# A decode step for a prompt and a sample group: the sample group's HGRN step among the compressed branch's tiles, its state products in float32, and page-table loads issued later

## The chip, the core and the metric

One core of a Trainium2 chip runs the whole kernel. The metric is device time in microseconds (us) of one execution. The engines are TensorE (PE in the profile), VectorE (DVE), ScalarE (ACT), GpSimd (POOL) and SyncE (SP); SP, ACT and POOL each have a queue from which DMAs are issued.

## What is computed

One layer of a hybrid decoder: eight attention heads with three branches (compressed blocks, selected blocks, window) beside four HGRN heads with a state of 128 x 128 each. It runs for a prompt of 1024 tokens and for a sample group of 8 sequences with one new token each and 1024 earlier tokens in paged caches. The step that the change moves is the sample group's HGRN step, one chunk of length 1:

```
f = lb + (1 - lb) * sigmoid(f_b);  k = (1 - lb) * sigmoid(-f_b)
q = silu(q_b);  v = i_b
S_new = f[k] * S + k (x) v          # (8 sequences, 4 heads, 128, 128)
o = q @ S_new
y_b = rmsnorm(o) * norm_w * silu(z_b)
```

The compressed branch reads the raw K and V rows of each sequence through the page table (`cache_cmp_kv[page_table]`), forms overlapping blocks of 32 rows and sends each through a small two-layer network:

```
flat = (blocks + pe).reshape(B, nc, KVH, 32 * 64)
k_c, v_c = silu(flat @ w1 + b1) @ w2
```

## The kernel before

The program is one long stream of operations; a scheduler of the framework places them into one instruction order for each engine, from data dependences, the buffers of pools and the order in which the code emits them. Each engine runs its order strictly, so an instruction that waits holds back all behind it. `after(a, b)` (L44) adds an order between two instructions without a semaphore.

The stages are: loading and normalising x (`load_x`), the projections (`project`), the compressed branch, the maxima and the branches of the prompt's attention, the sample group's attention, and the finish. A projection multiplies x by a 128-row tile of weights in three F32R products (high by high, low by high, high by low), `feat` with 344 streamed columns; `load_w` (L224) loads a tile `w_raw` through SP, ACT makes `w_hi` (L238) and DVE `w_lo` (L239).

Into the projections are laid the prompt's four HGRN heads. `hgrn_a` builds the decay-weighted products of Q and K in PSUM and copies them through masks into the tile AT on DVE (L490, L513, L520, L540); `hgrn_b` multiplies AT by V, carries the state and normalises O (L608 on POOL), which PE then transposes (L612).

The sample group's step is the generator `hgrn_sample` (L422 to L467). `go` lets it run two heads between `hgrn_a` and `hgrn_b` of head 3 and one after it. For each head it loads the state S for eight sequences (128 partitions x 1024) and vb, the new v spread over 128 partitions from the DRAM tile v_d, both through SP (L437, L439). DVE forms vb*k (L441), POOL S*f (L442), DVE the sum (L443), and SP stores the new state (L444). ACT and DVE then split S into a high and a low F32R half (S0h, S0l), and eight pairs of matmuls against qp, a zero tile with q of one sequence in one column, add up o in PSUM. After the last head o is normalised and transposed (L464). All its tiles lie in the pool of the HGRN stage (hp), which is closed at `hctx.close()` before the compressed branch can use the memory.

`page_index` (L645) loads the page table in eight small DMAs (pt_raw, L651; 16 partitions x 8 elements of 4 bytes each) and makes the row index pidx on DVE (L658), which the gathers read.

The compressed branch (`compress_setup`, `compress`, L666 to L755) loads nine tiles of raw rows into `cg`, two buffers of 128 x 2048: eight by indirect DMA on POOL (`gather`, L660), tile 8 from the DRAM tile kv_d by SP (L706). DVE and ACT copy each out of its slot (cr, L710). It goes through three groups of three tiles, eight steps each; a step has a turn (six transposes on PE, L717, a high and a low half x on ACT and DVE) and a multiplication with w1 (12 matmuls), and each turn stands one step ahead of its multiplication. POOL subtracts the low halves w1l of the weights (L51). Projections (`feat` C_Q, C_ZA, C_ZB) fill PE in between.

Of the kernel before, what the change touches and what calls it, by code (L numbers as in the profile page):

```python
# [20 lines left out]
NB = 8  # L21
# [6 lines left out]
class Kernel:  # L28
# [44 lines left out]
    def rsqrt(self, pool, y, x):  # L73
# [3 lines left out]
        t = pool.tile([128, n], F32, name="rs_t")[:p]  # L77
        g = pool.tile([128, n], F32, name="rs_g")[:p]
# [19 lines left out]
    def consts(self):  # L98
# [23 lines left out]
        self.vcS = cp.tile([64, NB + 1, 128], F32, name="vcS")  # L122
# [101 lines left out]
    def load_w(self, src, *parts):  # L224
# [4 lines left out]
        for k in range(8):  # L229
            raw = self.wpool.tile([128, 512], F32, name="w_raw", bufs=3)[:, :width]  # L230
            o = 0
            for c0, n in parts:
                dma = nc.sync.dma_start(raw[:, o:o + n], src[k * 128:(k + 1) * 128, c0:c0 + n])
                o += n
# [45 lines left out]
    def project(self, ctx):  # L280
# [24 lines left out]
        def ev_f(h0):  # L305
            def ev(f, ts, p):
# [8 lines left out]
                nc.vector.tensor_scalar(K[h][:, ts], K[h][:, ts], self.oml[:, h:h + 1], None, op0=OP.mult)  # L315
# [74 lines left out]
        for _ in smp:  # L390
            pass
# [30 lines left out]
    def hgrn_sample(self):  # L422

        nc, hp, a = self.nc, self.hp, self.a
# [3 lines left out]
        o = hp.tile([32, 128], F32, name="so", bufs=1)  # L428
        for h in range(4):
            yield  # L430
            po = self.ps_t.tile([128, 512], F32, name="pt")[:64, :128]
            qp = hp.tile([128, NB, 64], F32R, name="qp", bufs=1)
            nc.vector.tensor_scalar(qp.rearrange("p (a c) d -> p a (c d)", c=2), self.ones[:, None, :].to_broadcast([128, 4, 128]), 0.0, None, op0=OP.mult)
            qv = qp.rearrange("p b c -> p (b c)")
            self.split(qv[:, h * NB:h * NB + 456:65], qv[:, 32 + h * NB:32 + h * NB + 456:65], q[:, h], nc.vector, nc.vector)
            S = hp.tile([128, NB, 128], F32, name="S0", tag="S")
            nc.sync.dma_start(S, a["state_hgrn"][0, :, h].rearrange("b k v -> k b v"))  # L437
            vb = hp.tile([128, NB, 128], F32, name="vb", tag="O")
            nc.sync.dma_start(vb, bass.AP(tensor=v_d.tensor, offset=v_d.offset + h * 128, ap=[[0, 128], [512, NB], [1, 128]]))  # L439
# [5 lines left out]
            hi = hp.tile([128, NB, 128], F32R, name="S0h", tag="F")  # L445
            lo = hp.tile([128, NB, 128], F32R, name="S0l", tag="F")
            self.split(hi, lo, S, nc.scalar, nc.vector)
            for b in range(NB):
                self.mm(po, qp[:, b], hi[:, b], b == 0, False)
                self.mm(po[:32], qp[:, b, :32], lo[:, b], False, b == NB - 1)  # L450
            if h:
                nc.vector.tensor_tensor(o, o, po[:32], op=OP.add)
            else:
                nc.vector.tensor_copy(o, po[:32])
            nc.vector.tensor_tensor(o, o, po[32:], op=OP.add)
        sq = hp.tile([32, 128], F32, name="ssq", bufs=1)
# [188 lines left out]
    def page_index(self, pool):  # L645
# [749 lines left out]
```

## Time and profile before

| | us |
|---|---|
| three runs | 1084.05, 1085.75, 1096.07 |
| median | 1085.75 |
| the profiled execution | 1086.7 |
| its span | 1085.0 |
| PE busy in the span | 1047.7 |

The span is that from the first to the last instruction of the trace; 1.7 us of the profiled execution lie around it. Busy time of PE counts matmuls whose ends are modelled. "Granted clock" is the mean share of full speed that TensorE was given in a stretch. In the rows, `out<-in` names tiles, `xN` counts instructions, and an arrow in brackets names what ended the idle time before an instruction.

### The profile page before, as it was taken

The numbers are of one execution on the slowest core, as the hardware profiler recorded it, in microseconds if no ns is written. First come the engines' busy times: TensorE is split into PE (matmuls) and PEld (weight loads), VectorE is DVE, ScalarE is ACT, GpSimd is POOL, SyncE is SP. The second block draws the span as 40 slices with busy tenths as digits, with TensorE's granted clock in tenths as the row PEclk, the third lists the DMA queues.
The fourth block names the chain that finished last, engine by engine and source line by source line (L and its number), as shares of the span: only waits on it lengthen the run. The fifth ranks groups of instructions, "written<-read, shape, count | busy, mean of one in ns | idle before, by whom it ended". The sixth has DMA issues, their size and how long they took to land.

```text
span 1085.0 us, 18918 instructions
## 1 busy us (share of the span) xinstructions
PE 1047.7 (97%) x7021; PEld 933.6 (86%) x7021; DVE 617.8 (57%) x1822; ACT 388.4 (36%) x786; POOL 243.9 (22%) x276
## 2 busy tenths in 40 slices
PE   4999999999899999999989999999999999999998
PEld 3898799999889899999968888888788888778876
DVE  6847565665494634543665656766665686471223
ACT  4622234313132335432234544553554232241112
POOL 0014232331041133002032211121323133131111
PEclk9999999999989999999989999999999999999999
DMA  6212023323464766403568611001831573121110
GB/s 195 79 29 69 11 72 100 117 89 119 131 176 142 214 210 211 148 1 107 129 215 266 154 29 51 20 21 53 227 106 40 161 209 90 41 97 49 49 35 30
DMA packets 118815, 116.44 MB, mean 107 GB/s; under 512 B 18710, under 2 KB 100974, under 8 KB 116420
## 3 DMA queue, kind: packets, MB, share of 16 engines
q1 hardware_dynamic: 97220, 79.46, 25.7%
q10 hardware_dynamic: 19200, 19.01, 5.1%
q0 software_dynamic: 2304, 16.78, 4.5%
q8 instruction: 55, 0.90, 0.4%
q14 instruction: 36, 0.29, 0.1%
HBM read 84.84 MB, written 29.31 MB: 105 GB/s over the span
## 4 chain that ended last, share of the span: by engine, by line
PE 82%; DMA 9%; DVE 4%; issue 2%; ACT 2%; POOL 1%; SPq 0%; ACTq 0%; DVEq 0%; POOLq 0%
PE pa L42 39%; PE pb L42 26%; PE ph L42 9%; PE pt L42 4%; DMA vb<-v_d 2%; DMA w_raw<-w_in 2%; PE ph L717 1%; PE pa L1125 1%; DMA fw_raw<-w_out 1%; DMA fw_raw<-ple_gate 1%; DMA x_in<-x_prompt 1%; DVE fw_lo L51 1%; PE ph L1319 1%; DMA gpre<-g_pre 0%; DMA f_oa<-oa_d 0%
## 5 line engine op out<-in xcount | busy, mean ns | idle before, releaser
L42 PEld LDWEIGHTS pb<-V,P 128*128 128x128 f32 x1056 | 141.8, 191 | 12.1 <-POOL P L960 1.2
L42 PE MATMUL pb<-V,P 128*128 128x128 f32 x1056 | 148.1, 276 | 0.4 <-DVE mx L909 0.4
L42 PE MATMUL pa<-xhi,w_hi 128*128 128x344 f32 x384 | 126.0, 330 | 2.6 <-ACT w_hi L238 1.1
L42 PE MATMUL pa<-xlo,w_hi 128*128 128x344 f32 x384 | 124.5, 326 | 0.0
L42 PE MATMUL pa<-xhi,w_lo 128*128 128x344 f32 x384 | 123.5, 327 | 0.0
L955 ACT ACTIVATE P<-ph 128x512 f32<-128x512 f32 (+4 forms) x148 | 85.6, 595 | 98.6 <-PE ph L42 69.3
L916 DVE CUSTOM_DVE_ANT_0 junk<-pa,mask 128x320 bf16<-128x320 f32 (+5 forms) x150 | 72.9, 497 | 27.8 <-PE pa L42 26.6
L42 PE MATMUL pa<-w_lo,xhi 128*128 128x256 f32 (+2 forms) x256 | 79.5, 314 | 0.0
L42 PE MATMUL pa<-w_hi,xlo 128*128 128x256 f32 (+2 forms) x256 | 79.2, 314 | 0.0
L42 PE MATMUL pa<-w_hi,xhi 128*128 128x256 f32 (+2 forms) x256 | 78.6, 316 | 0.0
L42 PEld LDWEIGHTS pa<-xhi,w_hi 128*128 128x128 f32 x384 | 73.5, 192 | 4.2 <-ACT w_hi L238 1.7
L238 ACT ACTIVATE w_hi<-w_raw,gpre 128x512 fp32r<-128x512 f32 (+2 forms) x80 | 47.5, 616 | 78.2 <-DMA w_raw<-w_in 43.0
L42 PEld LDWEIGHTS pa<-xlo,w_hi 128*128 128x128 f32 x384 | 73.5, 192 | 0.1
L42 PEld LDWEIGHTS pa<-xhi,w_lo 128*128 128x128 f32 x384 | 73.0, 191 | 0.2
L42 PE MATMUL ph<-QA,KA 128*128 128x512 f32 (+4 forms) x148 | 66.7, 453 | 3.8 <-ACT P L955 2.9
L42 PE MATMUL pa<-KB,QB 65*128 65x320 f32 (+6 forms) x195 | 63.4, 363 | 0.1
L239 DVE SCALAR_TENSOR_TENSOR w_lo<-w_raw,gpre,w_hi 128x512 fp32r<-128x512 f32 (+2 forms) x80 | 50.6, 653 | 21.4 <-ACT w_hi L238 20.7
L42 PE MATMUL pa<-fw_hi,yh 128*128 128x512 f32 (+1 forms) x160 | 61.9, 387 | 0.2 <-ACT fw_hi L50 0.2
L42 PE MATMUL pa<-fw_lo,yh 128*128 128x512 f32 (+1 forms) x160 | 61.6, 385 | 0.0
L42 PE MATMUL pa<-fw_hi,yl 128*128 128x512 f32 (+1 forms) x160 | 61.6, 385 | 0.0
L42 PE MATMUL ph<-QB,KB 68*128 68x512 f32 (+4 forms) x148 | 58.5, 406 | 0.0
L559 POOL TENSOR_TENSOR K<-K,E 128x512 f32<-128x512 f32 x24 | 36.4, 1517 | 94.2 <-PE pb L42 57.2
(457 smaller groups left out, 2411.9 us busy)
## 6 DMA issues: line engine op xcount, KB each, us to landing
w_raw<-w_in SPq DMA_DIRECT2D x32, 256.0 KB
w_raw<-w_in SPq DMA_DIRECT2D x48, 128.0 KB
VS<-sg SPq DMA_DIRECT2D x8, 512.0 KB
sg<-cache_win_kv SPq DMA_DIRECT2D x16, 256.0 KB
fw_raw<-w_out SPq DMA_DIRECT2D x16, 256.0 KB
fw_raw<-ple_gate SPq DMA_DIRECT2D x16, 256.0 KB
f_x<-x_prompt SPq DMA_DIRECT2D x8, 512.0 KB
win_kv_sample<-cache_win_kv SPq DMA_DIRECT2D x8, 511.0 KB
```

The source lines that it names most:

```text
L42: return self.nc.tensor.matmul(out, lhsT, rhs, start=start, stop=stop, skip_group_check=True)
L51: lo_eng.tensor_tensor(lo, src, hi.bitcast(F32), op=OP.subtract)
L238: nc.scalar.activation(hi, raw, AF.Copy, scale=g)
L239: nc.vector.scalar_tensor_tensor(lo, raw, g, hi.bitcast(F32), op0=OP.mult, op1=OP.subtract)
L559: nc.gpsimd.tensor_tensor(Kv[:, :, 0], Kv[:, :, 0], Ev[:, :, 1:2].to_broadcast([128, nb, m]), op=OP.mult)
L717: nc.tensor.transpose(pt[:, i * 128:(i + 1) * 128], src[b0 + j // 2, kv][:, j % 2, 2 * jp:2 * jp + 2].rearrange("p j d -> p (j d)"), self. ...
L916: nc.vector.tensor_tensor_reduce(junk, pm, mk, 1.0, -1e30, op0=OP.add, op1=OP.max, accum_out=o)
L955: nc.scalar.activation(P, ps, AF.Exp, scale=0.125)
L1125: nc.tensor.transpose(pt[:, j * 128:(j + 1) * 128], rows(j), self.ident)
L1319: nc.tensor.transpose(pt[:, c], h[:, k * 128:(k + 1) * 128], self.ident[:n, :n])
```

## The change

Three things are done. First, the generator `hgrn_sample` is cut into `update` and `read` for a head, and these are called from the loop over the compressed branch's steps: update 0, update 1, read 0, read 1 at steps 1 to 4, and update 2, update 3, read 2, read 3 at steps 9, 10, 12 and 13; the normalisation follows after the last step. S and vb of a head lie together in one slot of `cg`, and both are loaded through POOL's queue (L440, L441). Second, S is no longer split: qp (32 columns, float32, in a slot of `w1r`) is multiplied with S itself, one float32 matmul for each of the eight sequences. Third, the eight page-table loads are ordered behind the last weight load of the i projection, and the making of pidx (now `page_rows`) behind the last K of the f projection (`lastf`).

```diff
@@ load_w
-                dma = nc.sync.dma_start(raw[:, o:o + n], src[k * 128:(k + 1) * 128, c0:c0 + n])
+                dma = self.lastw = nc.sync.dma_start(raw[:, o:o + n], src[k * 128:(k + 1) * 128, c0:c0 + n])
@@ project
         self.feat((C_FB + 256, 2, ev_f(2)))
+        self.page_rows()
         self.feat((C_QB + 256, 2, ev_q(2)))
-        go = lambda n: [next(smp, None) for _ in range(n)]
         for h in range(2, 4):
-            st = self.hgrn_a(h, Q[h], K[h], F[h])
-            go(2 if h == 3 else 0)
-            self.hgrn_b(h, *st)
-            go(1 if h == 3 else 0)
+            self.hgrn_b(h, *self.hgrn_a(h, Q[h], K[h], F[h]))
...
-        for _ in smp:
-            pass
...
             comp = self.compress()
-            for _ in range(5):
-                next(comp)
-            self.feat((C_Q, 4, ev_qa))
+
+            i = 0
             for _ in comp:
+                if i in (1, 2, 3, 4, 9, 10, 12, 13):
+                    next(smp, None)
+                if i == 4:
+                    self.feat((C_Q, 4, ev_qa))
+                i += 1
+            for _ in smp:
                 pass
@@ hgrn_sample
-        self.after(self.pidma, nc.sync.dma_start(v_d, self.vs))
+        self.after(nc.sync.dma_start(v_d, self.vs), self.pidma)
...
+        def update(h):
+            qp = hp.tile([128, 512], F32, name="w1r", bufs=2)[:, :32 * NB].rearrange("p (b c) -> p b c", c=32)
+            nc.gpsimd.memset(qp, 0.0)
+            nc.vector.tensor_copy(qp.rearrange("p b c -> p (b c)")[:, h * NB:h * NB + 232:33], q[:, h])
+            both = hp.tile([128, 2, NB, 128], F32, name="cg", bufs=2)
+            S, vb = both[:, 0], both[:, 1]
+            nc.gpsimd.dma_start(S, a["state_hgrn"][0, :, h].rearrange("b k v -> k b v"))
+            nc.gpsimd.dma_start(vb, bass.AP(tensor=v_d.tensor, offset=v_d.offset + h * 128, ap=[[0, 128], [512, NB], [1, 128]]))
             bc = lambda t: t[:, h, :, None].to_broadcast([128, NB, 128])
             nc.vector.tensor_tensor(vb, vb, bc(k), op=OP.mult)
             nc.gpsimd.tensor_tensor(S, S, bc(f), op=OP.mult)
             nc.vector.tensor_tensor(S, S, vb, op=OP.add)
             nc.sync.dma_start(a["hgrn_state_sample"][0, :, h].rearrange("b k v -> k b v"), S)
-            hi = hp.tile([128, NB, 128], F32R, name="S0h", tag="F")
-            lo = hp.tile([128, NB, 128], F32R, name="S0l", tag="F")
-            self.split(hi, lo, S, nc.scalar, nc.vector)
+            held[h] = qp, S
+
+        def read(h):
+            qp, S = held[h]
+            po = self.ps_t.tile([128, 512], F32, name="pt")[:32, :128]
             for b in range(NB):
-                self.mm(po, qp[:, b], hi[:, b], b == 0, False)
-                self.mm(po[:32], qp[:, b, :32], lo[:, b], False, b == NB - 1)
+                self.mm(po, qp[:, b], S[:, b], b == 0, b == NB - 1)
...
+        for step, h in ((update, 0), (update, 1), (read, 0), (read, 1), (update, 2), (update, 3), (read, 2), (read, 3)):
+            step(h)
+            yield
@@ page_index
             dma = nc.sync.dma_start(raw[16 * i:16 * i + 16], bass.AP(tensor=pt.tensor, offset=pt.offset + i, ap=[[0, 16], [8, NB]]))
+            self.after(dma, self.lastw)
...
-        nc.vector.scalar_tensor_tensor(self.pidx, raw, 16.0, lane, op0=OP.mult, op1=OP.add)
+        self.pages = raw, lane
+
+    def page_rows(self):
+
+        raw, lane = self.pages
+        self.after(self.nc.vector.scalar_tensor_tensor(self.pidx, raw, 16.0, lane, op0=OP.mult, op1=OP.add), self.lastf)
```

On DVE, in the HGRN stage of head 3, the order of before has the products of vb (L441) among the masked copies into AT (`z_s` is the evacuation of another projection, `PQl` a low half):

```order
L369 COPY z_s<-pa 128x256
L441 TENSOR_TENSOR vb<-vb,sfkq 128x1024
L520 COPY_PREDICATED AT<-lm_496,ph 128x512
L51 TENSOR_TENSOR PQl<-PQ,PQh 128x1024
L490 COPY_PREDICATED AT<-lm_495,pt 128x512
L369 COPY z_s<-pa 128x256 x2
L441 TENSOR_TENSOR vb<-vb,sfkq 128x1024
L513 COPY_PREDICATED AT<-lm_498,ph 128x256x2
```

and the changed kernel has at the same place (the copies into AT have line numbers higher by 7 there, z_s has L367):

```order
L367 COPY z_s<-pa 128x256
L527 COPY_PREDICATED AT<-lm_496,ph 128x512
L51 TENSOR_TENSOR PQl<-PQ,PQh 128x1024
L497 COPY_PREDICATED AT<-lm_495,pt 128x512
L367 COPY z_s<-pa 128x256
L520 COPY_PREDICATED AT<-lm_498,ph 128x256x2
L520 COPY_PREDICATED AT<-lm_497,ph 128x256x2
L367 COPY z_s<-pa 128x256
```

The two products of vb are gone from among the copies, and one copy z_s fewer stands ahead of the second pair of masked copies.

On POOL, at the start of the compressed branch, before (cg is a gathered tile, w1l the low half of a weight tile; the last four rows belong to the next stage):

```order
L662 DMA cg<-cache_cmp_kv,pidx 128x2048 x2
L51 TENSOR_TENSOR w1l_3789<-w1r,w1h_3788 128x512
L662 DMA cg<-cache_cmp_kv,pidx 128x2048
L51 TENSOR_TENSOR w1l_3789<-w1r,w1h_3788 128x512
L662 DMA cg<-cache_cmp_kv,pidx 128x2048
L51 TENSOR_TENSOR w1l_3789<-w1r,w1h_3788 128x512 x2
L51 TENSOR_TENSOR w1l_3807<-w1r,w1h_3806 128x512 x4
L662 DMA cg<-cache_cmp_kv,pidx 128x2048 x4
L818 MEMSET V_5375 128x32x64
L819 MEMSET vc_5376 64x2x64
L840 MEMSET mask 128x640
L847 MEMSET mkc 128x120
```

and now, from the second gather on:

```order
L675 DMA cg<-cache_cmp_kv,pidx 128x2048
L51 TENSOR_TENSOR w1l_3624<-w1r,w1h_3623 128x512
L440 DMA cg<-state_hgrn 128x8x128
L441 DMA cg<-v_d 128x8x128
L51 TENSOR_TENSOR w1l_3624<-w1r,w1h_3623 128x512 x2
L444 TENSOR_TENSOR cg<-cg,sfkq 128x1024
L51 TENSOR_TENSOR w1l_3642<-w1r,w1h_3641 128x512 x4
L436 MEMSET w1r 128x256 x2
L440 DMA cg<-state_hgrn 128x8x128
L441 DMA cg<-v_d 128x8x128
L444 TENSOR_TENSOR cg<-cg,sfkq 128x1024
L675 DMA cg<-cache_cmp_kv,pidx 128x2048 x3
```

The loads of S and vb of heads 0 and 1 stand among the gathers and the w1l, and the gathers of tiles 3 to 5, the last row, stand behind the second state's multiplication with f (L444). POOL's order goes on, that last row repeated first:

```order
L675 DMA cg<-cache_cmp_kv,pidx 128x2048 x3
L440 DMA cg<-state_hgrn 128x8x128
L441 DMA cg<-v_d 128x8x128
L444 TENSOR_TENSOR cg<-cg,sfkq 128x1024
L436 MEMSET w1r 128x256 x2
L440 DMA cg<-state_hgrn 128x8x128
L441 DMA cg<-v_d 128x8x128
L675 DMA cg<-cache_cmp_kv,pidx 128x2048
L444 TENSOR_TENSOR cg<-cg,sfkq 128x1024
```

Heads 2 and 3 follow the gathers of tiles 3 to 5, and tile 6 stands between the loads of head 3 and its multiplication; tile 7 comes behind these rows.

On DVE, near the first turns of the compressed branch, the changed kernel has (cr are copies out of a slot, x the low halves of a turn):

```order
L723 COPY cr_3680<-cg 128x1024
L353 TENSOR_TENSOR z_s<-pa,z_s 128x344 x2
L51 TENSOR_TENSOR x_3665<-ph,x_3664 128x2x192
L723 COPY cr_3686<-cg 128x1024
L51 TENSOR_TENSOR x_3667<-ph,x_3666 128x2x192
L443 TENSOR_TENSOR cg<-cg,sfkq 128x1024
L51 TENSOR_TENSOR x_3665<-ph,x_3664 128x2x192
L353 TENSOR_TENSOR z_s<-pa,z_s 128x344
L445 TENSOR_TENSOR cg<-cg 128x1024
```

Of these, the product of vb with k (L443) and the sum (L445) are new at this place; before, they stood in the HGRN stage.

## Rows read from the trace of the kernel before

**Rows 1.** The page: busy time by engine over the span, and the chain

```profile
PE 1047.7 (97%) x7021; PEld 933.6 (86%) x7021; DVE 617.8 (57%) x1822; ACT 388.4 (36%) x786; POOL 243.9 (22%) x276
...
PE 82%; DMA 9%; DVE 4%; issue 2%; ACT 2%; POOL 1%; SPq 0%; ACTq 0%; DVEq 0%; POOLq 0%
```

**Rows 2.** Windows: length; busy PE, PEld, DVE, ACT, POOL; granted clock; DMA share, GB/s

```profile
280.00:290.00 10.00, 7.93 (x58) 7.35 (x56) 2.98 (x5) 1.33 (x3) 0.00 (x0) 1.00 0.31 81
290.00:300.00 10.00, 6.22 (x44) 5.86 (x44) 5.02 (x7) 0.38 (x2) 0.00 (x0) 0.99 0.57 162
300.00:310.00 10.00, 9.33 (x53) 8.95 (x54) 8.76 (x11) 3.57 (x6) 5.50 (x3) 0.67 0.60 179
...
360.00:370.00 10.00, 7.43 (x40) 7.14 (x40) 4.44 (x8) 3.08 (x6) 2.85 (x1) 0.83 0.50 163
```

**Rows 3.** Waits of PE: engine and line, what it waited for, us in total, times, longest

```profile
PE ph L42 <- DVE AT L513: 3.6, 1, 3.6
...
PE ph L42 <- DVE AT L520: 2.9, 1, 2.9
...
PE pt L612 <- POOL O L608: 2.6, 1, 2.6
...
PE pa L42 <- ACT w_hi L238: 1.1, 2, 0.9
```

**Rows 4.** DVE: one wait, then timeline (start, us, operation, idle before, releaser)

```profile
DVE vb L441 <- DMA vb<-v_d: 16.1, 4, 5.3
...
288.37 1.23 DVE L441 TENSOR_TENSOR vb<-vb,sfkq 128x1024 f32<-128x1024 f32 x1 [5.26 <-DMA vb<-v_d]
289.51 1.28 DVE L520 COPY_PREDICATED AT<-lm,ph 128x512 f32<-128x512 uint8 x1
...
298.10 1.23 DVE L441 TENSOR_TENSOR vb<-vb,sfkq 128x1024 f32<-128x1024 f32 x1 [4.98 <-DMA vb<-v_d]
...
359.61 1.23 DVE L441 TENSOR_TENSOR vb<-vb,sfkq 128x1024 f32<-128x1024 f32 x1 [2.09 <-DMA vb<-v_d]
```

**Rows 5.** Timeline of the start: the queue of SP, and one wait of ACT

```profile
16.85 3.27 SPq L651 DMA_DIRECT2D pt_raw<-page_table  x7
...
27.96 0.72 ACT L238 ACTIVATE w_hi<-w_raw,gpre 128x512 fp32r<-128x512 f32 x1 [6.01 <-DMA w_raw<-w_in]
```

**Rows 6.** Timeline of PE: projection, float32 product, first and last of 16 state products

```profile
309.60 0.32 PE L42 MATMUL pa<-xlo,w_hi 128*128 128x344 f32 x1
309.75 1.95 PE L42 MATMUL pb<-Q,K 128*128 128x128 f32 x16
...
381.78 0.22 PE L42 MATMUL pt<-S0h,qp 128*64 128x128 f32 x1
...
382.68 0.22 PE L42 MATMUL pt<-S0l,qp 128*32 128x128 f32 x1
```

**Rows 7.** Compressed branch: timeline of POOL, then the operations on the gathered tile cg

```profile
392.55 1.17 POOL L662 DMA_INDIRECT cg<-cache_cmp_kv,pidx  x1 [11.50 <-PE pt L464]
...
420.09 2.68 POOL L51 TENSOR_TENSOR w1l<-w1r,w1h 128x512 fp32r<-128x512 f32 x2 [2.32 <-ACT w1h L50]
...
L710 ACT COPY cr<-cg x9: 1032/1052/1058, 399.4 to 475.8; 128x1024 f32<-128x1024 f32 x9
L662 POOL DMA_INDIRECT cg<-cache_cmp_kv,pidx x8: 939/946/1168, 392.6 to 453.2; - x8
...
DMA to landing us min/median/max: 5.5/7.0/9.2
```

**Rows 8.** State tile S: its multiplication on POOL (ns min/median/max, first and last start)

```profile
L442 POOL TENSOR_TENSOR S<-S,sfkq x4: 1898/1900/2495, 300.1 to 354.4; 128x1024 f32<-128x1024 f32 x4
```

**Rows 9.** Windows in and after the compressed branch, columns as in rows 2

```profile
440.00:450.00 10.00, 10.00 (x72) 9.57 (x71) 5.58 (x12) 4.66 (x10) 0.94 (x1) 1.00 0.32 108
540.00:550.00 10.00, 8.30 (x43) 6.84 (x42) 8.26 (x35) 2.93 (x5) 4.39 (x10) 0.95 0.42 116
550.00:560.00 10.00, 8.35 (x31) 5.98 (x29) 8.04 (x33) 4.52 (x8) 2.01 (x6) 0.54 1.06 354
```

More of the change, by code (lines that the diff above doesn't have):

```diff
@@ L71, in packed, with rsqrt @@
         return t
-    def rsqrt(self, pool, y, x):
+    def rsqrt(self, pool, y, x, p0=0):
         nc = self.nc
         p, n = x.shape
-        t = pool.tile([128, n], F32, name="rs_t")[:p]
-        g = pool.tile([128, n], F32, name="rs_g")[:p]
+        t = pool.tile([128, n], F32, name="rs_t")[p0:p0 + p]
+        g = pool.tile([128, n], F32, name="rs_g")[p0:p0 + p]
         nc.vector.tensor_scalar(t.bitcast(I32), x.bitcast(I32), 1, None, op0=OP.logical_shift_right)
@@ L121, in consts @@
         self.oml = cp.tile([128, 4], F32, name="oml")
-        self.vcS = cp.tile([64, NB + 1, 128], F32, name="vcS")
+        self.vcF = cp.tile([128, NB + 1, 128], F32, name="vcS")
+        self.vcS = self.vcF[:64]
         self.G = cp.tile([128, 8, 24], F32, name="G")
@@ L314, in ev @@
                                         op0=OP.mult, op1=OP.add)
-                nc.vector.tensor_scalar(K[h][:, ts], K[h][:, ts], self.oml[:, h:h + 1], None, op0=OP.mult)
+                self.lastf = nc.vector.tensor_scalar(K[h][:, ts], K[h][:, ts], self.oml[:, h:h + 1], None, op0=OP.mult)
             return ev
@@ L422, in hgrn_sample @@
     def hgrn_sample(self):
-        nc, hp, a = self.nc, self.hp, self.a
+        nc, a = self.nc, self.a
         f, k, q = (self.sfkq[:, i] for i in range(3))
         v_d = self.dram.tile([NB, 512], F32, name="v_d")
-        self.after(self.pidma, nc.sync.dma_start(v_d, self.vs))
[L428 to L439, printed above, removed]
+        self.after(nc.sync.dma_start(v_d, self.vs), self.pidma)
+        yield
+        hp = self.zp
+        o = self.vcF[64:96, 0]
+        held = {}
+        def update(h):
[6 more added lines that the diff above has]
+            nc.gpsimd.dma_start(vb, bass.AP(tensor=v_d.tensor, offset=v_d.offset + h * 128, ap=[[0, 128], [512, NB], [1, 128]]))
             bc = lambda t: t[:, h, :, None].to_broadcast([128, NB, 128])
@@ L444, in hgrn_sample @@
             nc.sync.dma_start(a["hgrn_state_sample"][0, :, h].rearrange("b k v -> k b v"), S)
-            hi = hp.tile([128, NB, 128], F32R, name="S0h", tag="F")
-            lo = hp.tile([128, NB, 128], F32R, name="S0l", tag="F")
-            self.split(hi, lo, S, nc.scalar, nc.vector)
+            held[h] = qp, S
+        def read(h):
+            qp, S = held[h]
+            po = self.ps_t.tile([128, 512], F32, name="pt")[:32, :128]
             for b in range(NB):
-                self.mm(po, qp[:, b], hi[:, b], b == 0, False)
-                self.mm(po[:32], qp[:, b, :32], lo[:, b], False, b == NB - 1)
+                self.mm(po, qp[:, b], S[:, b], b == 0, b == NB - 1)
             if h:
-                nc.vector.tensor_tensor(o, o, po[:32], op=OP.add)
+                nc.vector.tensor_tensor(o, o, po, op=OP.add)
             else:
-                nc.vector.tensor_copy(o, po[:32])
-            nc.vector.tensor_tensor(o, o, po[32:], op=OP.add)
-        sq = hp.tile([32, 128], F32, name="ssq", bufs=1)
-        ss = hp.tile([128, 1], F32, name="sr", bufs=1)[:32]
+                nc.vector.tensor_copy(o, po)
+        for step, h in ((update, 0), (update, 1), (read, 0), (read, 1), (update, 2), (update, 3), (read, 2), (read, 3)):
+            step(h)
+            yield
+        sq = hp.tile([128, 512], F32, name="w1r", bufs=2)[64:96, :128]
+        ss = hp.tile([128, 1], F32, name="sr", bufs=1)[64:96]
         nc.scalar.activation(sq, o, AF.Square, accum_out=ss)
         nc.vector.tensor_scalar(ss, ss, 1.0 / 128, EPS, op0=OP.mult, op1=OP.add)
-        r = hp.tile([128, 1], F32, name="srs", bufs=1)[:32]
-        self.rsqrt(hp, r, ss)
-        nc.vector.tensor_scalar(o, o, r, None, op0=OP.mult)
+        r = hp.tile([128, 1], F32, name="srs", bufs=1)[64:96]
+        self.rsqrt(hp, r, ss, 64)
+        on = hp.tile([128, 512], F32, name="w1r", bufs=2)[:32, :128]
+        nc.vector.tensor_scalar(on, o, r, None, op0=OP.mult)
         pt = self.ps_t.tile([128, 512], F32, name="pt")[:, :32]
-        nc.tensor.transpose(pt, o, self.ident[:32, :32])
-        oT = hp.tile([128, 32], F32, name="soT", bufs=1)
+        nc.tensor.transpose(pt, on, self.ident[:32, :32])
+        oT = hp.tile([128, 512], F32, name="w1r", bufs=2)[:, :32]
         nc.scalar.copy(oT, pt)
```

## The prediction

> **What bounds the kernel now.** I read the page first, then windows of 10 us over the whole span, then PE's waits, then the timelines of the engines that PE waited for. The page shows a kernel bound by PE: 1047.7 of 1085.0 us busy, and PE holds 82% of the chain that ended last [rows 1]. So only two things pay: gaps in PE, and PE's own instructions. The gaps are few, 37.3 us in all (1085.0 less 1047.7). The windows show that four of them lie together, in the HGRN stage of head 3: PE is idle 2.07, 3.78, 0.67 and 2.57 us in the stretches that begin at 280, 290, 300 and 360 us, 9.1 us in all [rows 2]. The last column but two matters as much: the granted clock was 0.67 in the third and 0.83 in the fourth, so 3.3 and 1.7 us of full-speed work were lost there on top. Of the two levels of 1.2 and 2.4 GHz, 0.67 is a mean, and it comes right after 3.6 us in which PE did nothing.
>
> What PE waited for has three names: the masked copies of L520 and L513 into AT on DVE (2.9 and 3.6 us), and the scaled O of L608 on POOL (2.6 us) [rows 3]. None is slow itself. DVE's timeline shows what stood ahead of them: the product vb*k of L441, which had waited 5.26 and 4.98 us for the DMA that loads vb, with the masked copy queued behind it [rows 4]. The fourth vb, at 359.61, stood the same way ahead of the last small operation before L608. DVE waited 16.1 us for the four vb loads; all of PE's 9.1 idle us follow from them.
>
> **The change part by part.** Durations are those of the profiled execution: 1086.7 us, 1.7 us above its span and 0.95 us above the median of 1085.75. I sum against 1086.7 and take off 0.95 at the end.
>
> (1) The sample group's step leaves the HGRN stage. The masked copies now follow the work before them directly, as the order rows show. At most 9.1 us idle and 5.0 us of clock come back, 14.1 us. What is late next there is not visible: DVE was busy only 2.98 and 5.02 of 10 us in the two worst windows, so it has room, and it loses this step's operations. I leave 1 us to the next wait: -13, with -9 (the clock not regained, or other waits in its place) and -14.1 as ends.
>
> (2) Its products on PE. Before, 16 F32R matmuls a head, from 381.78 to 382.68 plus one spacing of 0.06: 0.96 us, for four heads 3.8 us. After, 8 float32 matmuls a head. The trace has no float32 matmul of 32 by 128; the nearest row is Q,K of 128 by 128, eight matmuls that stand as 16 in the profile and take 1.95 us [rows 6]. Narrower weights may load faster, so 0.96 is the lower end and 1.95 the upper; I take 1.85, since the 128 streamed columns are the same. Four heads: 7.4 less 3.8, +3.6 (0 to +4). The copies and subtractions for the high and low halves on ACT and DVE go as well; neither engine is the bound, so they count nothing.
>
> (3) The page-table loads. Seven of them took SP 3.27 us from 16.85, ahead of five pairs of weight loads, and ACT then waited 6.01 us for a weight tile at 27.96 [rows 5]. PE had work meanwhile: only 1.1 us of its waits are put down to w_hi [rows 3]. So -1.1, between 0 and -2. Their new place is behind the last i weights, and what they delay on SP are weights needed tens of us later; the index itself is first used by the gathers past 360 us. I count nothing for that; without this cover it would cost the same 3.3 us.
>
> (4) The new waits in the compressed branch, the term that decides. There is little idle there to hide in: PE was busy for 10.00 of 10 us from 440 on, as in nearly every window of the branch [rows 9]. The step's S and vb now take one of the two slots of cg, which the gathers need, and both are loaded from POOL. So the nine tiles and the four states form one chain through two slots: tile 3 waits until state 0 is read and stored, tile 4 until state 1 is read, the states 2 and 3 wait until tiles 4 and 5 are copied, tiles 6 and 7 wait for the reads of 2 and 3, and tile 8 for the copies of tile 6.
>
> I follow the chain from the first gather, called 0. It starts earlier than before, as it need not wait 11.5 us for the sample group's last transpose [rows 7]; PE fills that time with projections. An issue takes 0.95 us, landing 7.0 (5.5 to 9.2), a copy out of the slot up to 1.05 [rows 7], S*f on POOL 1.9 [rows 8]. POOL's last w1l subtraction ended 30.2 us after the first gather before (420.09 + 2.68 - 392.55); two loads and one S*f now stand among them, so state 1 is loaded from about 34, multiplied by 44; tile 3 is gathered then, tile 4 after read 1. PE's place I count in its rows of the new order at 0.155 to 0.165 us each (projections, from 309.60 to 309.75 [rows 6], with a little for 384 columns): the first product of the branch at 31, read 1 at 50 to 52, the turn that needs tiles 3 to 5 at 62, read 3 at 88 to 90, the turn that needs tiles 6 to 8 at 92. Tiles 4 and 5 are ready at about 60, just in time. State 3, which POOL loads only behind the S*f of state 2, is added up at 84, before its read. But tile 7 is gathered after read 3, at 90: 90 + 7.0 + 1 = 98 against 92. Tile 8, loaded when tile 6 has been copied at 87, comes at 97. PE waits 4 to 6 us there. I take 5, and 2 more for clock (3.6 us of idling cost 3.3 us in rows 2) and small waits at the first turns: +7, from 2 (the fastest landing, no loss of clock) to 12.
>
> What a plain load from POOL costs the trace does not show. Nearest is the gather, 0.94 to 1.17 us for 128 rows, though each of these loads has 1024 pieces of 512 bytes. The lower end is that of the gather; the upper, eight times as many pieces, 7.5 us. I take 1.1, the row nearest in kind. POOL issued none of them before, so nothing can be gained there.
>
> Here the Trainium skill can be weighed, "DMA: Bandwidth & Descriptors", section "Anatomy of one DMA — SWDGE (gpsimd) path". It says that one can emit many descriptors before the added cost shows; by it the sum stays as it is. The same page's section "SWDGE vs HWDGE vs iDMA" speaks against the change: descriptors written by GpSimd are held up while VectorE runs in a mode that locks the shared port. The gathers at 0.939 to 1.168 us [rows 7] ran beside DVE copies and show none of it; were it to hold, the loads would be those of rival B below.
>
> (5) The stage after the branch. The float32 maxima there leave PE waiting for DVE: in the windows at 540 and 550 it is idle 1.70 and 1.65 us, with clock 0.54 in the second [rows 9]. PE's filler is the last projection; about 40 of its rows (6.3 us) now run earlier, under the branch, and are missing at the end of this stage. They are not lost, since they fill the branch; I put +1, from 0 to +5.
>
> Sum: -13 + 3.6 - 1.1 + 7 + 1 = -2.5. 1086.7 - 2.5 = 1084.2, less 0.95: 1083 us. A measurement of this kernel can tell about 1%, 10.9 us, from no change; the forecast is within that.
>
> **The rivals.** (A) The gap goes and no new one comes: tiles 7 and 8 land in 5.5 us, or the order leaves PE filler at that turn. For it: POOL, DVE and ACT are far from full, and PE's queue still has projections. Against: the chain has no slack at tile 7, whose gather cannot start before read 3. Price: -14.1 + 2 (narrower products, half way to the lower end) - 1.1 + 2 + 0 = -11.2, so 1086.7 - 11.2 - 0.95 = 1074.6 us.
>
> (B) The other side: POOL's loads are dear, and the two slots decide. One mechanism, at the third turn: state 3 can be loaded only behind state 2's loads and S*f, so each us of issue above 1.1 is paid up to four times between tile 4 and read 3. There are about 4 us of slack, so it decides from some 3 us a load. At 4 us tiles 4 and 5 are 4 late, state 3 another 11, and tile 7 again 5, with 5 of clock: 25 in place of 7, 1083 + 18 = 1101 us. For it: eight times the pieces of a gather. Against: nothing in the gathers' rows grows with DVE or DMA load.
>
> (C) The change does less than it says in the HGRN stage: another late operation takes vb's place in DVE's queue (-5 instead of -13): 1091 us. Against it speak DVE's idle shares.
>
> (D) The filler is missed in full after the branch (+5 instead of +1): 1087 us.
>
> **How the numbers follow.** Forecast case 0.40, A 0.25, B 0.17, C 0.08, D 0.10. A lies on the border of 1% (1074.9): most of it, 0.21, counts as faster, with 0.04 of the forecast case: 0.25. B counts as slower but for 0.02; with 0.03 of C and 0.02 of D: 0.20. The rest, 0.55, is no change. Range 1071 to 1099: A with its best ends below, most of B above. The likeliest case's own range is 1077 to 1090 (terms 1 and 4 at half their way to the ends).
>
> **What would show it.** Right: no DVE wait for vb ahead of AT in the HGRN stage and clock 1.00 there; a PE wait of 4 to 6 us for ph at the turn with tiles 6 to 8, its releaser a copy from cg; 16 rows of pt from cg a head in about 1.9 us; POOL's loads near 1 us. Wrong: loads of 3 us or more, PE waits at the second turn or at reads, or a gap in the HGRN stage that another name ends.

## The result, and the profile after

| | before | after |
|---|---|---|
| median of 6 runs each, us | 1087.24 | 1098.64 |
| ratio, 95% interval | | 1.0099 (1.0071 to 1.0127) |
| profiled execution, us | 1086.7 | 1099.06 |
| its span, us | 1085.0 | 1097.4 |
| mean clock of the run, median | 0.989 of 95 runs | 0.983 of 14 runs |

The change made the kernel slower by 1.0%: the forecast of 1083 us had the wrong sign, and the time lies at the upper end of its range. (The 95 runs of before are those timed beside the experiments below, the 14 of after those of two series.)

The page of after answers to [rows 1]. PE is 11.6 us busier, and `issue` in its chain has gone from 2% to 4%:

```profile
PE 1059.3 (97%) x7021; PEld 940.2 (86%) x7021; DVE 611.8 (56%) x1806; ACT 386.2 (35%) x782; POOL 248.1 (23%) x288
...
PE 80%; DMA 9%; DVE 4%; issue 4%; ACT 2%; POOL 0%; SPq 0%; ACTq 0%; DVEq 0%; POOLq 0%
```

The number of matmuls is the same, so part of those 11.6 us is the same work at a lower clock. PE's idle time, the span less its busy time, is nearly what it was, 37.3 us before and 38.1 now: what the HGRN stage gave back was lost again in other places. Windows show where. They are cut at the six stretches in which PE ever waits for long (start; i projection; HGRN stage; compressed branch; maxima; late branches); columns as in [rows 2]. Before:

```profile
0.00:60.00 60.00, 43.70 (x251) 40.11 (x252) 41.88 (x183) 31.47 (x60) 3.70 (x13) 1.00 0.41 124
60.00:120.00 60.00, 60.00 (x313) 52.56 (x312) 36.24 (x50) 15.54 (x26) 20.99 (x16) 1.00 0.15 44
275.00:365.00 90.00, 80.91 (x655) 78.38 (x655) 52.72 (x98) 21.57 (x54) 20.50 (x16) 0.96 0.52 153
365.00:500.00 135.00, 134.50 (x885) 130.23 (x884) 61.30 (x140) 56.77 (x114) 18.74 (x20) 0.99 0.45 145
500.00:600.00 100.00, 96.65 (x615) 87.50 (x614) 58.35 (x204) 32.88 (x64) 24.17 (x57) 0.95 0.68 196
740.00:860.00 120.00, 117.36 (x809) 101.28 (x808) 76.47 (x362) 52.01 (x92) 35.49 (x53) 1.00 0.41 114
```

After:

```profile
0.00:60.00 60.00, 45.70 (x275) 43.60 (x276) 41.55 (x183) 32.39 (x61) 3.69 (x13) 1.00 0.41 124
60.00:120.00 60.00, 57.04 (x281) 48.80 (x280) 34.85 (x46) 14.49 (x24) 20.27 (x15) 0.97 0.15 44
275.00:365.00 90.00, 90.00 (x720) 88.30 (x720) 43.91 (x89) 26.33 (x63) 10.28 (x17) 1.00 0.37 120
365.00:500.00 135.00, 127.35 (x817) 119.49 (x816) 64.37 (x135) 48.42 (x99) 35.49 (x32) 0.99 0.53 165
500.00:600.00 100.00, 96.42 (x591) 86.08 (x590) 54.39 (x202) 31.51 (x60) 24.70 (x56) 0.90 0.66 178
740.00:860.00 120.00, 116.64 (x805) 101.95 (x805) 73.42 (x348) 51.91 (x92) 35.19 (x53) 0.96 0.35 98
```

Two numbers of a row make its price: idle is the length less PE's busy time, lost clock is the length times (1 less the granted clock). The clock has two digits, so its price can be off by some 0.5 us. Set against the terms of the forecast, in us:

| term | forecast | profile | from |
|---|---|---|---|
| (1) HGRN stage | -13 | -14.1 | idle 9.1 to 0, clock 5.0 to 0 (3.6, and 1.4 behind 365 us) |
| (2) float32 products | +3.6 | +3.9 | 4 heads x (1.93 - 0.96), row below |
| (3) page loads | -1.1 | +2.8 | start: idle 16.3 to 14.3; 60 to 120: idle +3.0, clock +1.8 |
| (4) compressed branch | +7 | +8.6 | idle 0.5 to 7.7, clock 0 to 1.4 |
| (5) stage after it | +1 | +5.2 | idle +0.2, clock 5 to 10 |
| late branches | not named | +5.5 | idle +0.7, clock 0 to 4.8 |
| sum | -2.5 | +11.9 | spans differ by 12.4 |

The 1.4 us of clock that before loses between 365 and 500 us lie at 365 to 370 us (clock 0.69), right behind the wait for O, so they are counted in (1). This is one profile of each kernel; the second pair, under "The clock" below, differs in the last two terms.

In the HGRN stage the 10-us windows of [rows 2] now read 10.00 busy of 10 and a clock of 1.00 at 280, 290 and 300 us, and none of the waits of [rows 3] for AT or O is left. The longest new ones of after:

```profile
PE ph L730 <- DVE x L51: 3.3, 2, 2.8
PE ph L42 <- ACT PRh L50: 3.0, 1, 3.0
...
PE ph L730 <- DVE cr L723: 2.1, 2, 1.5
...
PE pb L42 <- DVE x L51: 1.4, 1, 1.4
```

The second is the page loads. Timelines of SP, ACT and PE there (start, us, operation, idle before and releaser), which answer to [rows 5] (`win_kv_sample` is a copy of cached rows to an output):

```profile
80.14 1.28 SPq L245 DMA_DIRECT2D win_kv_sample<-cache_win_kv  x2
81.45 4.93 SPq L658 DMA_DIRECT2D pt_raw<-page_table  x8
86.48 2.17 SPq L234 DMA_DIRECT2D w_raw<-w_in  x3
...
94.68 0.51 ACT L239 ACTIVATE w_hi<-w_raw,gpre 128x256 fp32r<-128x256 f32 x1 [7.50 <-DMA w_raw<-w_in]
...
95.56 0.62 ACT L50 CAST PRh<-PR 128x512 fp32r<-128x512 f32 x1
...
96.23 0.50 PE L42 MATMUL ph<-PRh,ones 128*128 128x512 f32 x1 [2.96 <-ACT PRh L50]
```

The loads hold SP for 4.93 us, the next weight tile lands late, ACT waits 7.50 us for it, and behind ACT's w_hi stands PRh (the high half of a tile of the prompt's HGRN heads), which PE needs at once.

The first and last kind of wait are one mechanism. DVE and PE in the compressed branch:

```profile
452.27 1.23 DVE L443 TENSOR_TENSOR cg<-cg,sfkq 128x1024 f32<-128x1024 f32 x1 [3.42 <-DMA cg<-v_d]
453.42 0.55 DVE L51 TENSOR_TENSOR x<-ph,x 128x384 fp32r<-128x384 f32 x1
...
454.02 0.55 PE L730 MATMUL ph<-ident,cr 128*128 128x128 f32 x3 [2.78 <-DVE x L51]
```

DVE stands 3.42 us for the load of vb of head 3, with the low half x of a turn queued behind it: the same picture as [rows 4], with x in the place of AT. The operations on cg, with the landing times, and the products of one head:

```profile
L675 POOL DMA_INDIRECT cg<-cache_cmp_kv,pidx x8: 937/992/1590, 365.8 to 459.0; - x8
L440 POOL DMA_DIRECT2D cg<-state_hgrn x4: 925/941/975, 379.1 to 443.7; - x4
L441 POOL DMA_DIRECT2D cg<-v_d x4: 884/912/927, 380.1 to 444.6; - x4
L444 POOL TENSOR_TENSOR cg<-cg,sfkq x4: 1893/1894/1899, 386.3 to 448.6; 128x1024 f32<-128x1024 f32 x4
...
DMA to landing us min/median/max: 4.8/6.9/9.2
...
402.24 1.93 PE L42 MATMUL pt<-cg,w1r 128*32 128x128 f32 x16
```

### The profile page after: what moved, and what is told of

The parts are those of the page before. It is cut to its first block, busy times and chain, and to the rows that moved or that the text cites. A ratio compares the mean times of both kernels' runs of the same rounds, so it can differ in the third digit from the quotient of the medians.

```text
span 1097.4 us, 18884 instructions
## 1 busy us (share of the span) xinstructions
PE 1059.3 (97%) x7021; PEld 940.2 (86%) x7021; DVE 611.8 (56%) x1806; ACT 386.2 (35%) x782; POOL 248.1 (23%) x288
## 4 chain that ended last, share of the span: by engine, by line
PE 80%; DMA 9%; DVE 4%; issue 4%; ACT 2%; POOL 0%; SPq 0%; ACTq 0%; DVEq 0%; POOLq 0%
PE pa L42 36%; PE pb L42 26%; PE ph L42 9%; PE pt L42 4%; DMA fw_raw<-w_out 2%; DMA cg<-v_d 2%; DMA w_raw<-w_in 1%; PE ph L730 1%; PE pa L1138 1%; DMA cg<-cache_cmp_kv,pidx 1%; DMA fw_raw<-ple_gate 1%; DVE fw_lo L51 1%; PE ph L219 1%; PE ph L1332 1%; DMA V<-x_prompt 1%
## 5 line engine op out<-in xcount | busy, mean ns | idle before, releaser
L42 PEld LDWEIGHTS pb<-V,P 128*128 128x128 f32 x1056 | 147.4, 197 | 13.0 <-PE ph L42 0.8
L42 PE MATMUL pb<-V,P 128*128 128x128 f32 x1056 | 153.4, 283 | 0.5 <-DVE mx L922 0.4
L240 DVE SCALAR_TENSOR_TENSOR w_lo<-w_raw,gpre,w_hi 128x512 fp32r<-128x512 f32 (+2 forms) x80 | 55.3, 709 | 25.6 <-ACT w_hi L239 23.9
L566 POOL TENSOR_TENSOR K<-K,E 128x512 f32<-128x512 f32 x24 | 33.6, 1401 | 113.9 <-PE pb L42 54.0
```

Of the source, the lines that this page charges most:

```text
L42: return self.nc.tensor.matmul(out, lhsT, rhs, start=start, stop=stop, skip_group_check=True)
L240: nc.vector.scalar_tensor_tensor(lo, raw, g, hi.bitcast(F32), op0=OP.mult, op1=OP.subtract)
L566: nc.gpsimd.tensor_tensor(Kv[:, :, 0], Kv[:, :, 0], Ev[:, :, 1:2].to_broadcast([128, nb, m]), op=OP.mult)
```

## The experiments

Theory after the result: the work came out near the forecast; what failed is the place of the page loads, and the clock. Rivals: the reads (the step's products on PE) or POOL's loads are dear, the late normalisation holds the maxima, or the clock differs by chance.

**The page part.** Undone in the changed kernel (loads at the head of SP again, index made with them):

```diff
-        self.page_rows()
...
-            self.after(dma, self.lastw)
...
+        nc.vector.scalar_tensor_tensor(self.pidx, raw, 16.0, lane, op0=OP.mult, op1=OP.add)
```

> The changed kernel with the page-table loads and the index put back where they were before. Theory: in the changed kernel their new place stops SP for 4.9 us at 81 us, the next weight tile comes late, ACT's w_hi waits 7.5 us with PRh queued behind it, and PE loses 3 us of idling and 1.5 of clock; at the start the new place gained 3.8. So undoing it costs 3.8 at the start and gives 4.5 to 5.3 back at 96 us: 0.5 to 1.5 us less than the changed kernel, no PE wait for PRh, start of the projections 3.8 us later. Rival, as I had forecast: the new place is a plain gain, and undoing it costs 1 to 4 us.

Measured: 1095.77 us, ratio 1.0078 (1.0050 to 1.0107). The wait for PRh is gone and the start idles 17.1 us again; the gain on the changed kernel has the sign of the theory, but is not clear of noise, as the intervals overlap. Next, the loads of the changed kernel issued later, behind the second f weights, together with the beginning of the step (the store of v_d):

```diff
-        self.page_index(self.cp)
-        smp = self.hgrn_sample()
-        next(smp)
...
         self.feat((C_FB + 256, 2, ev_f(2)))
+        self.page_index(self.cp)
+        smp = self.hgrn_sample()
+        next(smp)
         self.page_rows()
```

> The changed kernel with the page-table loads emitted behind the second f weights instead of the i weights, so that SP issues them when the weights of the next projection are already on their way. Theory of the SP queue: the gain of 3.8 us at the start stays and the 4.5 to 5.3 us at 96 us go, so 4 to 5 us less than the changed kernel, about 1094 us, and no PE wait of 3 us for PRh. Rival, that the wait at 96 us has another cause (ACT's order): no change, within 1 us.

Measured: 1092.82 us, 1.0035 (1.0017 to 1.0053); the wait for PRh is gone, the start stays shorter, and a wait of 1.7 us for Q is new. And the page part alone, put on the kernel before (the diff's third part):

> The kernel before with only the page-table part of the change. Theory: minus 3.8 us at the start, plus 4.5 to 5.3 at 96 us: +0.5 to +1.5 us against before, with the wait for PRh. Rival, as forecast: -1 to -4 us.

Measured: 1091.25 us, 1.0020 (0.9986 to 1.0055), with a wait for PRh of 3.4 us. So the idea is sound (the start gains 2 us) and the place chosen is wrong: the same loads further on are 5.8 us better (1098.64 less 1092.82; the intervals do not overlap), of which the profile of after names about 4.8 (3.0 idle, 1.8 clock).

**The float32 reads alone**, on the kernel before (qp becomes float32 too):

```diff
...
-            self.split(hi, lo, S, nc.scalar, nc.vector)
             for b in range(NB):
-                self.mm(po, qp[:, b], hi[:, b], b == 0, False)
-                self.mm(po[:32], qp[:, b, :32], lo[:, b], False, b == NB - 1)
+                self.mm(po, qp[:, b], S[:, b], b == 0, b == NB - 1)
```

> The kernel before with only the float32 products on the unsplit state, at their old place. The changed kernel shows 16 rows in 1.93 us a head, twice the 0.96 of before, so PE gets 3.9 us of work. If only PE counts: +3.9 us. Rival: in the HGRN stage DVE and ACT are the late ones, and 4 casts of 1.05 us and 4 subtractions of 1.2 us go from them, which can give some of the 14 us gap back: 0 or below.

Measured: 1092.64 us, 1.0022 (0.9999 to 1.0045), 2.4 us of 1089; 1.93 to 1.94 us a head. The term stands; that less than 3.9 us reached the end fits the rival of the expectation, as the HGRN stage idles 6.5 us in its profile (9.1 before), but the interval does not tell the two apart.

**The step left out**, in the kernel before and in the changed one (o is zero, no new states are stored; the edit of the changed one):

```diff
+        nc.vector.memset(o, 0.0)
...
-            step(h)
             yield
```

> The kernel before without the four heads of the step; o is set to zero and the new states are not stored. It gives the cost of the step at its old place: 3.9 us of PE for the products, 9.1 us of waits and 5 of clock if the gap is the vb loads' alone: 14 to 18 us less than before, about 1071 to 1074. Rival, that without vb another operation of DVE or POOL is late for AT: 5 to 10 us less. Where both kernels without the step differ, it is by the page-table part, 1 to 4 us, and by the late normalisation.

> The changed kernel without the four updates and reads of the sample group's HGRN step; o is set to zero and the new states are not stored, the normalisation stays. What it is faster than the changed kernel by is the cost of the step in the compressed branch. Theory from the trace: 7.7 us of PE for the reads, 7.5 us of PE waits in the branch, about 2 of clock: 15 to 19 us less, about 1080 to 1084. Rival, that the branch's waits stay without the step (gathers and weights late by themselves): only 8 to 10 us less.

Measured: 1084.46 us, 0.9966 (0.9935 to 0.9997), and 1082.84 us, 0.9930 (0.9907 to 0.9953). In its old place the whole step, gap and products, cost 0.34%, 3.7 us (by the interval 0.3 to 7.1); in the new one 1.0099 less 0.9930, 1.7%, some 18 us (16 by the medians). In the trace of before without it PE is some 17 us ahead at 368 us (one and the same projection product starts at 368.25 us, and in before at 385.31) and then waits for the first gathered tile:

```profile
373.90 0.69 PE L693 MATMUL ph<-ident,cr 128*128 128x128 f32 x2 [5.33 <-DVE cr L686]
```

With the low clock of the maxima, where it loses 10 us for 5, it is only 3.4 us ahead at the end (spans 1081.6 and 1085.0). That gap was worth much less than its own length. Nor is the clock that of one profile: the six runs without the step have mean clocks of 0.985 to 0.987, below the 0.989 of before, though nothing of the change is in them: the step is only left out.

**The normalisation earlier**, at step 15 in place of after the loop, alone and together with the later page loads:

```diff
-                if i in (1, 2, 3, 4, 9, 10, 12, 13):
+                if i in (1, 2, 3, 4, 9, 10, 12, 13, 15):
```

> The changed kernel with the normalisation of the sample group's o emitted at step 15 of the compressed branch instead of after its last step; nothing else differs. Theory: in the changed kernel its last small operations (transpose, copy, store of oT) end at 506 us and hold the branch's memory, so that POOL's zeroing of V begins at 508.3 instead of 500.6 and SP's st loads at 508.8 instead of 496.7; the maxima start some 8 us late, PE's filler is used up before them, and PE loses about 5 us at 540 to 570, most of it as clock. Then this kernel starts V and st near 500 and is 3 to 6 us faster than the changed one, about 1093 to 1096. Rival: those 5 us are only where PE happens to be when the clock falls: no change beyond 1.5 us, though V starts earlier.

> The changed kernel with the page-table loads behind the second f weights and the normalisation at step 15. If both causes add: 4 to 6 us for the first and 3 to 6 for the second, so 1087 to 1091, level with before. Rival (the second is worth nothing): 1093.

Measured: 1097.80 us, 1.0084 (1.0055 to 1.0113), and 1094.20 us, 1.0058 (1.0037 to 1.0079). The memset of V and the first maxima come earlier (the maxima 3.2 us behind before in place of 7.4), and the end does not move: the late normalisation is not the cause.

**DVE out of the wait**, on top of these two edits:

```diff
-            nc.vector.tensor_tensor(vb, vb, bc(k), op=OP.mult)
             nc.gpsimd.tensor_tensor(S, S, bc(f), op=OP.mult)
-            nc.vector.tensor_tensor(S, S, vb, op=OP.add)
+            nc.gpsimd.tensor_tensor(vb, vb, bc(k), op=OP.mult)
+            nc.gpsimd.tensor_tensor(S, S, vb, op=OP.add)
```

> The changed kernel with the later page index and the early normalisation, and with the product vb*k and the sum moved from DVE to POOL, so that DVE no longer stands waiting for vb with x behind it. Theory (PE's waits in the compressed branch come from DVE held by vb): the two waits for x, 2.8 and 2.9 us in the kernel with the two edits, fall below 1 us together, the windows there return to a clock of 1.00, and the median falls from 1094.2 to about 1087 (1084 to 1090). Rival (the two slots of cg are the limit, DVE is held only because the load is late): the wait goes on under another name, a copy cr or the read of a state, and the median stays at 1091 or more.

Measured: 1090.27 us, 1.0006 (0.9973 to 1.0039): 3.9 us less than without it (the intervals just touch). The two long waits for x (2.9 and 2.8 us) became five of at most 1.3. The branch before the edit and after it (here with PE's busy time alone, then clock):

```profile
365.00:500.00 135.00, 126.63 (x803) 0.97 0.53 162
```

```profile
365.00:500.00 135.00, 129.55 (x833) 0.99 0.53 165
```

Idle fell from 8.4 to 5.4 us and lost clock from 4.1 to 1.4. More than half of the idle stays, so DVE held by vb is about one half of the branch's price, idle and clock; the rest is shorter waits for x and one of 1.3 us for the DMA of a small tile (pe_t). This is the best version with the step in the branch; it is not faster than the kernel before, though level with it: these edits take back the whole 1%.

**The same in the old place**: vb*k, the sum and S0l of the kernel before on POOL.

```diff
-            nc.vector.tensor_tensor(vb, vb, bc(k), op=OP.mult)
+            nc.gpsimd.tensor_tensor(vb, vb, bc(k), op=OP.mult)
...
-            self.split(hi, lo, S, nc.scalar, nc.vector)
+            self.split(hi, lo, S, nc.scalar, nc.gpsimd)
```

> The kernel before with its step where it was, but with vb*k, the sum and the low halves S0l on POOL in place of DVE. Theory (the gap in the HGRN stage is DVE held by vb; but little of it reaches the end, as the kernel before with the step left out was only 3.7 us faster): the waits for AT, 3.6 and 2.9 us, go, PE is 9 to 13 us ahead by 371 us, and the median falls by 0 to 4 us only, 1084 to 1088. Rival (a gap of 9.1 us of idle and 5.0 us of clock is worth its whole price, 14 us): 1077 or less. A third way: POOL held by vb holds O of the third or fourth head, and the gap stays under that name: 1087 to 1092.

Measured: 1089.50 us, 1.0012 (0.9977 to 1.0048). The waits for AT are gone, but qp on DVE (3.0 us) and K on POOL (2.3) took their place, and the HGRN stage still idles 6.9 us: the third way of the expectation.

**The clock.** Both kernels again, unchanged, for a second profile.

> The kernel before, unchanged, for a second profile. Theory (the length of the low clock in the maxima stage belongs to the kernel): again about 10 us below 0.8 between 540 and 570 us, and every window of 10 us from 740 to 850 us at 1.00. Rival (it differs from one execution to the next): a spell of 15 us or more, or losses after 740 us, in the same program. About 1088 us in both cases.

> The changed kernel, unchanged, for a second profile. Theory (the length of the low clock belongs to the kernel): again about 20 us of low clock in the maxima stage, and windows at 0.83 to 0.95 between 740 and 850 us. Rival (it differs from one execution to the next): about 10 us in the maxima stage, or 1.00 after 740 us. What must stay in both cases are the waits of PE that the program's order makes: PRh near 96 us (about 3.0 us) and x near 454 us (about 2.8 us). About 1098 us, 1094 to 1101.

Measured: 1089.54 us, 1.0003 (0.9974 to 1.0032), and 1098.85 us, 1.0088 (1.0059 to 1.0117). The second profile of before, in the maxima and the late branches:

```profile
500.00:600.00 100.00, 97.23 (x585) 0.90 0.65 185
740.00:860.00 120.00, 116.39 (x808) 0.97 0.40 109
```

That is a loss of 10 and 3.6 us where the first profile lost 5 and 0, though PE's matmuls of the maxima came within 0.3 us of the first profile's up to 553 us, with the same waits to within 0.5 us. PE's windows of 5 us (its busy time, then clock), first profile, then second:

```profile
545.00:550.00 5.00, 3.30 (x12) 0.90 0.75 197
555.00:560.00 5.00, 5.00 (x19) 0.57 1.10 318
560.00:565.00 5.00, 5.00 (x36) 1.00 0.35 84
```

```profile
545.00:550.00 5.00, 3.42 (x10) 0.72 0.80 213
555.00:560.00 5.00, 5.00 (x17) 0.50 1.10 319
560.00:565.00 5.00, 5.00 (x17) 0.50 0.33 81
565.00:570.00 5.00, 5.00 (x30) 0.73 0.01 3
```

The low clock lasts from about 549 to 559 us in the one and from about 547 to 567 us in the other. The second profile of after, with the waits for PRh (3.6 us) and x (4.1) again:

```profile
500.00:600.00 100.00, 95.88 (x585) 0.90 0.63 172
740.00:860.00 120.00, 116.13 (x828) 0.99 0.36 98
```

It lost 10 us in the maxima again, but only 1.2 in the late branches. So the length of the low clock differs between executions of one program. The two second profiles are only 4.2 us apart (spans 1092.3 and 1096.5): PE's idle time is again the same (39.2 and 39.9 us), its busy time 3.5 us more, about the products, and the clock no lower. The +5.2 and +5.5 of the table are thus in part the luck of one profile of before. It is still not chance alone: 10 of the 95 runs of before, but 13 of the 14 of after, have a mean clock of 0.986 or less.

Does the low clock follow PE's waits there? The last products of the early maxima were done four times each:

```diff
-                        self.mm(pm, QB[:65, hh], keys, True, True)
+                        for _ in range(4 if self.early and self.npart > 20 else 1):
+                            self.mm(pm, QB[:65, hh], keys, True, True)
```

> The changed kernel; the last twelve or so of the early products of the maxima (KB,QB after the 20th) are done four times into the same tile, some 36 products more of about 0.16 us, 6 us, where PE waits for DVE between 546 and 556 us. Theory (the low clock of about 20 us, 10 us lost, follows the 3.6 us of scattered waits there): idle in 500 to 600 us falls below 2 us, the loss of clock there below 5 us, and the median comes to 1093 to 1098 although PE does 6 us more. Rival (the low clock does not come from these waits, or the maxima are set by DVE and lose their time anyway): the loss stays at 9 to 10 us and the median rises to 1101 or more.

> The kernel with the later page index, the early normalisation and the step's VectorE work on POOL, with the same repeated products. Theory: loss of clock in 500 to 600 us below 5 us (10 before), median 1084 to 1090, not above the 1090.3 without the repeats. Rival: the loss stays at 9 to 10 us and the median rises to 1093 or more.

Measured: 1096.89 us, 1.0069 (1.0042 to 1.0096), and 1092.30 us, 1.0042 (1.0017 to 1.0067). The maxima of the first, then of the second:

```profile
500.00:600.00 100.00, 98.87 (x626) 0.93 0.64 178
```

```profile
500.00:600.00 100.00, 98.21 (x623) 0.97 0.66 191
```

Idle fell from 3.6 to 1.1 and from 3.1 to 1.8 us, lost clock from 10 to 7 and to 3. The changed kernel became no slower in spite of some 36 products more. That speaks for the waits as a cause, but 7 is above the bound that was set, single profiles differ by as much, the profile of the second kernel is that of its fastest run, and its median rose by 2.0 us: not settled.

Last, the gap put back in the changed kernel: loads of two states and of vb through SP and two products vb*k among the masked copies of head 3, their results unused.

```diff
+            for j in range(2 if h == 3 else 0):
...
+                nc.sync.dma_start(vb, bass.AP(tensor=self.v_d.tensor, offset=self.v_d.offset + j * 128, ap=[[0, 128], [512, NB], [1, 128]]))
+                nc.vector.tensor_tensor(vb, vb, self.sfkq[:, 1][:, j, :, None].to_broadcast([128, NB, 128]), op=OP.mult)
```

> The changed kernel with the gap of the HGRN stage put back and nothing else of the old step: two loads of a state and of vb through SP and two products vb*k on DVE, among the masked copies of head 3 as before the change; their results are not used. PE must wait there again, 5 to 7 us for AT, with about 3 us of clock. Theory (the clock that the removed gap gave back is lost again in later stages: over the kernels run so far the loss after 500 us is about 7 us where the gap is there, 11 to 14 us where it is gone): the loss outside 275 to 365 us falls by some 4 us, the mean clock stays near 0.983, and the median rises by the idle time alone, to 1103 to 1106. Rival (the losses of the stages add up): the loss outside stays, the mean clock falls to about 0.980, and the median rises by idle and clock, to 1107 to 1111.

Measured: 1100.39 us, median of 4 runs, 1.0099 (1.0060 to 1.0138). Its profiled execution, 1106.7 us, shows the gap back and the loss in the maxima as large as ever:

```profile
275.00:365.00 90.00, 84.32 (x670) 0.98 0.40 125
...
500.00:600.00 100.00, 95.92 (x571) 0.88 0.56 152
```

In this trace the losses add up, against the theory; the median rose by less than either expected, 1.8 us, and the ratio not at all (1.0099). That fits what the kernel without the step showed, that a gap in this stage costs little at the end. The theory's own count does not hold either: in the maxima and late branches f32_alone and the second profile of before lost 12.6 and 13.6 us with the gap there, and other kernels 3 to 19 with it gone. Undecided.

## Why the prediction was wrong

Of its terms, three came out in their size. (1) The gap of the HGRN stage went as reasoned, -14.1 for -13, and nothing took its place there; what failed is that this gain was summed as if it reached the end (below). (2) The products cost 1.93 us a head, where 1.85 was taken from the row of Q,K. (4) The branch costs +8.6 for +7 (7.2 of idle time and 1.4 of clock, for a wait of 5 and 2 of clock and small waits), but by another way: PE waited 0.6 us, not 4 to 6, at the turn with tile 8, and 5.7 us for x behind the products of vb (two waits) and for cr at the first turn. DVE's order, with L443 ahead of x, was among the rows that the forecast was made from, but it followed the two slots instead of that queue; the size was luck. POOL's loads took 0.88 to 0.98 us against 1.1, so rival B falls. The Trainium skill ("DMA: Bandwidth & Descriptors", "Anatomy of one DMA — SWDGE (gpsimd) path") says that many descriptors can be emitted before the added cost shows; the trace agrees, with loads in 1024 pieces at 0.94 us beside gathers of 128 rows at 0.99.

Step (3) failed by its sign. "What they delay on SP are weights needed tens of us later ... I count nothing for that" looked at when PE needs the weights. But ACT takes them in its own order, and the wait for one weight tile also held PRh. The cost was 4.8 us at 60 to 120 us against 2.0 gained at the start. The prediction had the same rule in the other direction: it read [rows 5] as SP holding ACT.

The larger error is the clock. The forecast regained 5.0 us of it in the HGRN stage and put 2 against it. The mean clock of the runs instead fell from 0.989 to 0.983: 1.7% of 1097 less 1.1% of 1085, some 7 us more lost. With 3.9 us for the products and idle time that stayed the same, this is about the whole of the measured 11 us. The first pair of profiles places it at 90 to 100 us (1.8, explained by the page loads), in the maxima and in the late branches (5 and 4.8); the second pair does not show the last two. Term (5) named the stage and its idle time rightly (+0.2 us), and missed its clock: windows of after at 550 us read 0.50 where [rows 9] had 0.54, and the low spell lasts to about 570 us, not 560.

What lowers the clock in nearly all runs of the changed kernel is open. Shown is that one program has short and long spells, that it is not the late normalisation, and that it fell (to 0.986) when the step with its gap was only left out of the kernel before. Fewer waits in the maxima went with a smaller loss in two profiles; the second profile of before lost 10 us with no more idle time there than the first (2.8 and 3.4 us). With the page loads later and DVE's share of the step on POOL the runs' median clock is 0.988, nearly that of before.

Could the change have paid at all? Without the step, before gained 3.7 us, and the changed kernel is 7.6 us faster than before (0.9930). The step's products alone take PE 3.8 us in the one and 7.7 us in the other. A placement that hides all but the products would by these numbers have gained nothing, and some 4 us with the cheaper products of before (an estimate: 7.6 less 3.8); 14 us in [rows 2] was the price of a gap in its stage, not at the end.

## What to carry to other kernels

Before a gap is worked on, leave out what makes it and time that: here a gap of 9.1 us idle and 5.0 us of clock was worth 3.7 us at the end, with the products of the step in it. When a load moves along a queue, follow each tile behind it to the engine that converts it, and then to what is queued behind that instruction; a transfer "needed later" can hold an engine now. When an operation that waits for a DMA is moved to another stage, it takes its trouble along: look what stands behind it in the new place, and give it to an engine that nobody waits for.

## What the runs showed of the hardware

Two executions of one program, with PE's matmuls equal within 0.3 us up to 553 us, lost 5 and 10 us in the maxima: the low clock (0.50, the lower of the two levels) lasted some 10 us in one and 20 us in the other, with PE busy for most of the longer spell. Eight page-table loads of 128 elements each hold SP for 4.93 us, 0.62 us each, about as long as each of the two copies of 511 KB ahead of them (1.28 us for both), and POOL issues a load of 512 KB in 0.94 us: what a DMA costs its queue is not told by its bytes. The product of a 128 x 32 float32 weight with 128 columns takes as long as that of a 128 x 128 one (1.93 us for eight, against 1.95).
